# A hybrid encoder block on one core: casts and loads around the FFN's borders queued anew

## The chip, the cores and the metric

The kernel runs on one core of a Trainium2 chip. A core has five engines with a queue of instructions each: TensorE (PE in the profile, its weight loads PEld) multiplies matrices from SBUF into the PSUM banks; VectorE (DVE), ScalarE (ACT) and GpSimd (POOL) work elementwise; SyncE (SP) only issues DMA transfers. An engine takes its own instructions in the order in which the program was laid out; between engines, semaphores order them. The metric is the device time of one execution in microseconds, lower is better.

## The reference

One layer over 2048 tokens of width 1024, all in float32. Cut to what matters here:

```
h = rms_norm(x, pre_mix_g);  proj = h @ w_in
y_a = chunk_band_attention(q, k, v, rel_bias)
y_b = rwkv7_time_mix(p_rwkv, ...)
merged = sigmoid(gate_a) * (y_a @ proj_a) + sigmoid(gate_b) * (y_b @ proj_b)
x = x + rms_norm(merged @ w_out, post_mix_g)

hf = rms_norm(x, pre_ffn_g)
u = square(relu(hf @ w_up)) @ w_down        # 1024 -> 4096 -> 1024
x = x + rms_norm(u, post_ffn_g)
```

The change lies around the last four lines and the end of the line with w_out.

## The kernel before

**Splitting.** Each float32 operand of a matmul is split into a high part and a rest: `split` (L77) casts the high part on ACT (L78) and subtracts it from the source on DVE (L79). `split_here` (L1212) does the same with the rest left in the source's place (L1214, L1215). `mm3` multiplies high by high, high by rest and rest by high, three matmuls of 512 columns for each 128 rows of the contraction. So before PE can use an operand, a DMA has to land, a cast of 128x1024 has to run on ACT and a subtraction of the same size on DVE.

**Phases.** Four groups of 512 tokens go one after the other through the projections, the recurrence, attention and `phase_merge` (L1100). Then come two halves of 1024 tokens through the FFN: `phase_up`, `phase_down`, `phase_up`, `phase_down`.

**Merge.** `phase_merge` makes eight gated tiles: a product of 12 matmuls into a PSUM bank of the pool `pd` (two banks), its gating on DVE (`branch`, L1097), the sum with the other branch (L1114) and the split into `mh` and `ml` (L1115). The gate `th` comes by DMA into one of three buffers. Then `m @ w_out` runs in two halves of 512 columns (n = 0 and 1): eight steps k of 12 matmuls each into four banks, and at the end of a half ACT squares each bank (L1136) and DVE scales it by the norm row (L1137), after which the bank is free. The weights of w_out come as `wraw`, one load for two steps k.

**First activations.** `first_half` (L1218) loads the first token group's normalised activations for the FFN in four parts (`bl`) and splits them into `bh` and `bl`. For the first half it stands in the program behind the last merge, for the second half it is the last thing that the first `phase_down` advances beside its own work; there its casts are queued behind `self.second`, the weight cast of step 1.

**Up.** The FFN's two products use a form with seven block products in place of eight. `phase_up` (L1229) first runs eight blocks (`early`), each with a weight load, a split by `parts` (L1273) into one of the buffers a1, s12 and s3, a product A11 x B11 whose bank ACT copies to `z` (L1303), and a product A12 x B21 whose bank DVE adds to it (L1281); ACT then applies relu and square (L1282, L1283). Each product has 12 matmuls. Beside them the generator `operands` (L1251) loads and splits the five combined activations t2, t3, t1, b22 and t4 (two parts each), which the main loop needs. The main loop makes 16 passes; each splits S1 and S2 into s12, S3 and A22 into s3 and S4 into s4, and multiplies in the order S2, S3, S1, S4, A22. For passes below `early` the two first products exist already. The third block of the first half is the "third weights" of the title.

**Down.** `phase_down` (L1354) runs 56 steps, seven products of eight steps each; every step s needs one hidden block (`xraw`) and one weight block (`wdraw`), 512 KB each, from `operands(s)`, which is called two steps ahead. A step has 24 matmuls (L1409). `final` (L1426) closes a tile of 128 tokens: it loads the row tile `x1r` (two buffers), squares, scales by the norm row `gt` (a `gain` of 512 KB, L135), takes the root on POOL and adds. It is advanced from the sixth product on. The residual of the last token group (`residual`, L1140) runs beside the first down phase.

**Order.** The program is written in one order, but the order in each engine's queue is laid out at compile time by a planner: it takes an instruction as soon as, by its own estimates of time, its operands and buffers are ready and its engine is free, and prefers the one that stands earlier in the program. So a load, cast or subtraction of a later phase can be queued ahead of work that stands before it. `queue_behind(ins, first)` (L92) adds an edge for that planner alone: `ins` is laid out behind `first`. It adds no semaphore.

Of the kernel before, what the change touches and what calls it, by code (L numbers as in the profile page):

```python
# [18 lines left out]
P = 128  # L19
# [34 lines left out]
class Block:  # L54
# [79 lines left out]

    def gain(self, pool, src, name, bufs=1):  # L135
        t = pool.tile([P, D], F32, tag="gain", bufs=bufs, name=name)
        self.nc.sync.dma_start(t, src[None, :].to_broadcast((P, D)))
        return t

    def transpose_split(self, pt, src, hi, lo, tok, pinned=False):  # L140
# [959 lines left out]
    def phase_merge(self, g, o, op, between, beside):  # L1100

        tc, nc, a = self.tc, self.nc, self.a
        with ExitStack() as ctx:
            e = ctx.enter_context
            cp = e(tc.tile_pool(name="mgc", bufs=1, reuse_waits="tile"))
            po = e(tc.tile_pool(name="mgpo", bufs=4, space=PSUM, reuse_waits="tile"))
            mh = cp.tile([P, KB, G], F32R, name="mh")
            ml = cp.tile([P, KB, G], F32R, name="ml")
            gp = self.gain(op, a["post_mix_g"], "g_post")
            for i in range(KB):  # L1110
                mb = self.bp.tile([P, G], F32, tag="mb", bufs=3, name="mb")
                nc.sync.dma_start(mb, self.md[i])
                t = self.branch(self.ya, 0, i)
                nc.vector.tensor_tensor(t, t, mb, ALU.add)  # L1114
                self.split(mh[:, i], ml[:, i], t)  # L1115
            self.yctx.close()
            for n in range(2):
                ps = [po.tile([P, 512], F32, tag="o", name="ps_o") for _ in range(GT)]
                for k in range(KB):
                    if k % 2 == 0:  # L1120
                        w = a["w_out"][k * P : (k + 2) * P, n * 512 : (n + 1) * 512]
                        wh, wl = self.wsplit(w.rearrange("(j p) n -> p j n", p=P), "w", 2, 512)
                    for t in range(GT):
                        ts = slice(t * P, (t + 1) * P)
                        for j, (l, r) in enumerate(((mh, wh), (mh, wl), (ml, wh))):
                            nc.tensor.matmul(  # L1126
                                ps[t], l[:, k, ts], r[:, k % 2], start=k == 0 and j == 0, stop=k == KB - 1 and j == 2
                            )
                    if n == 0 and k in ((2, 4, 5, 6, 7) if g + 1 < self.NG else (0, 2, 3, 4, 5)):
                        advance(beside, 1)  # L1130
                    if n == 0 and k == 4 or n == 1 and k % 2 == 0:
                        advance(between, 1)
                ns = slice(n * 512, (n + 1) * 512)
                for t in range(GT):
                    sq = op.tile([P, 512], F32, tag="sqo", bufs=2, name="sqo")
                    nc.scalar.activation(sq, ps[t], AF.Square, accum_out=self.ssq[:, g, t, n : n + 1])  # L1136
                    nc.vector.tensor_tensor(o[t][:, ns], ps[t], gp[:, ns], ALU.mult)  # L1137
            advance(between)

    def residual(self, g, mp, bank):  # L1140
# [77 lines left out]
    def first_half(self, g, bp):  # L1218

        bh, bl = self.b1 = [bp.tile([P, KB, G], F32R, tag="b" + x, name="b" + x) for x in "hl"]  # L1220
        for k in range(0, KB, 2):
            ks = slice(k, k + 2)
            self.nc.sync.dma_start(bl[:, ks].bitcast(F32), self.ht[g][:, ks])
            high = self.split_here(bh[:, ks], bl[:, ks])
            if g:
                self.queue_behind(high, self.second)
            yield

    def phase_up(self, half, zp, rp, cb, pn, early):  # L1229
# [6 lines left out]
        with ExitStack() as ctx:  # L1236
# [14 lines left out]
            def operands():  # L1251
                td, g1 = self.td[half], self.ht[2 * half + 1]
                for n, src in (
# [3 lines left out]
                    for k in (0, 2):  # L1257
                        ks = slice(k, k + 2)
                        nc.sync.dma_start(l[:, ks].bitcast(F32), src[:, ks])
                        self.split_here(h[:, ks], l[:, ks])  # L1260
                        yield

            def product(l, r, pool, tag):
# [35 lines left out]

            ops = operands()  # L1300
            for i in range(early):
                A11, A12 = parts(load(2 * i), ("a1", "s12", "s3")[i % 3], KB)
                nc.scalar.copy(z[:, i], product(A11, B11, self.pd, "d"))  # L1303
                first(i, z[:, i])
                advance(ops, 1 + i % 2)
            advance(ops)

            last = None
# [45 lines left out]
    def phase_down(self, half, zp, rp, cb, pn, beside_of):  # L1354
# [4 lines left out]
        with ExitStack() as ctx:  # L1359
# [21 lines left out]
            def operands(s):  # L1381
# [5 lines left out]
                if isinstance(w, int):  # L1387
                    nc.sync.dma_start(wr, self.wd[w][f])
                else:
                    nc.sync.dma_start(wr, wrows[w[0]][:, 2 * f : 2 * f + 2, w[1]])  # L1390
                self.split(t[:, 0], t[:, 1], xr)
                high = self.split(t[:, 2], t[:, 3], wr)
                if s == 1:
                    self.queue_behind(self.relu, high)
                    self.second = high
                return t

# [28 lines left out]
            def final(t):  # L1426
                th = t // GT
                g, ts = gs[th], slice((t % GT) * P, (t % GT + 1) * P)
                x = op.tile([P, D], F32, tag="x", name="x1r")
                nc.sync.dma_start(x, self.x1[g][ts])  # L1430
                ssq = op.tile([P, 2], F32, tag="ssq", bufs=4, name="ssqu")
                for n in (1, 0):
                    ns = slice(n * G, (n + 1) * G)
# [19 lines left out]
            for s, (q, x, w, f) in enumerate(steps):  # L1453
# [9 lines left out]
                    continue  # L1463
                if s == NS - 3 * NF // 4 + 1:
                    gt = self.gain(op, a["post_ffn_g"], "g_post2")
                for t in range(GT):
                    down(ps[t], t, o, f == 0, f == NF // 4 - 1)
                    if f == NF // 4 - 1:
# [109 lines left out]
```

## Time and profile before

| | |
|---|---|
| median of 3 runs | 3269.18 us (3267.48 to 3270.03) |
| the profiled execution | 3272.55 us |
| its span, first to last instruction | 3270.8 us |
| mean granted clock of TensorE | 0.993 |
| first matmul of the first down phase | 2335.0 us |
| DMA moved | 592.54 MB, 181 GB/s over the span |

A line of the profile names the source line, the engine, the operation and the tiles as out<-in, with shapes and the number of instructions; a timeline line starts with the start and the duration in microseconds and ends, in brackets, with the idle time of the engine before the instruction and what ended it. Line numbers of helpers such as L78, L79 and L88 serve many callers, so tiles tell them apart: `a1h`, `s12h` and `s3h` are the split weights of the up phase, `t2h` to `t4h` and `b22h` its five operands, `bh` and `bl` the first activations, `fop` the operands of the down phase, `whi` and `wlo` the weights before the FFN.

### The profile page before, as it was taken

How to read it: one execution, taken by the hardware profiler on the slowest of the kernel's cores; microseconds unless marked ns; L12 is line 12 of the kernel's file. 1: busy time of each engine (PE TensorE's matmuls, PEld its weight loads, DVE VectorE, ACT ScalarE, POOL GpSimd, SP SyncE). 2: the span in 40 equal slices, each digit the busy share in tenths (PEclk: the TensorE clock that was granted, in tenths of full speed). 3: DMA queues.
4: the chain of work that ended last, by engine and by line, in shares of the span. 5: the costliest groups of instructions: out<-in, count | busy, mean ns of one | idle time of the engine just before them, and what ended most of it. 6: DMA issues, size and time to landing. Idle time of an engine off the chain costs nothing. (4 is left out here: it accounts for less than half of the span.)

```text
span 3270.8 us, 50026 instructions
## 1 busy us (share of the span) xinstructions
PE 3184.3 (97%) x18913; PEld 2599.2 (79%) x18913; DVE 2239.5 (68%) x3655; ACT 1576.9 (48%) x2511; POOL 596.0 (18%) x1101
## 2 busy tenths in 40 slices
PE   8999999999999999999999999999999999999998
PEld 6777778777888777878877887888888878888887
DVE  7785666776776785776866775887656768775464
ACT  5434635445745434755434653544543444544343
POOL 2221012122112222112222110122211212120000
PEclk9999999999999999999999999999999999999999
DMA  5245373246574236565336547654777875456565
GB/s 167 85 135 172 126 241 119 72 142 235 181 234 133 88 120 234 182 205 170 94 97 206 182 156 238 226 182 166 254 278 248 290 238 193 167 177 229 193 217 175
DMA packets 432282, 592.54 MB, mean 181 GB/s; under 512 B 25300, under 2 KB 295840, under 8 KB 432040
## 3 DMA queue, kind: packets, MB, share of 16 engines
q1 hardware_dynamic: 373928, 408.94, 39.9%
q0 software_dynamic: 48896, 163.61, 13.7%
q10 hardware_dynamic: 9216, 16.78, 1.4%
q8 instruction: 149, 2.44, 0.3%
q14 instruction: 93, 0.76, 0.1%
HBM read 425.37 MB, written 167.01 MB: 181 GB/s over the span
## 5 line engine op out<-in xcount | busy, mean ns | idle before, releaser
L1409 PE MATMUL ps_dn<-fop 128*128 128x512 f32 x2688 | 611.9, 389 | 1.8 <-DVE fop L79 1.7
L1409 PEld LDWEIGHTS ps_dn<-fop 128*128 128x128 f32 x2688 | 504.0, 188 | 107.8 <-DVE fop L79 2.8
L78 ACT CAST whi<-wraw 128x1024 fp32r<-128x1024 f32 x232 | 243.5, 1050 | 392.9 <-PE psd L88 301.1
L88 PE MATMUL psd<-hh,whi 128*128 128x512 f32 x1344 | 370.3, 403 | 10.7 <-DVE QA L894 10.7
L79 DVE TENSOR_TENSOR wlo<-wraw,whi 128x1024 fp32r<-128x1024 f32 x232 | 283.0, 1220 | 133.3 <-ACT whi L78 70.0
L88 PE MATMUL psd<-hl,whi 128*128 128x512 f32 x1344 | 367.2, 401 | 0.0
L88 PE MATMUL psd<-hh,wlo 128*128 128x512 f32 x1344 | 358.4, 398 | 0.0
L88 PEld LDWEIGHTS psd<-hh,whi 128*128 128x128 f32 x1344 | 244.8, 190 | 59.8 <-issue 11.8
L88 PEld LDWEIGHTS psd<-hl,whi 128*128 128x128 f32 x1344 | 249.1, 190 | 49.5
L88 PEld LDWEIGHTS psd<-hh,wlo 128*128 128x128 f32 x1344 | 247.9, 189 | 50.8 <-issue 1.4
L79 DVE TENSOR_TENSOR fop<-xraw,fop 128x1024 fp32r<-128x1024 f32 x112 | 137.0, 1224 | 178.9 <-ACT fop L78 178.7
L78 ACT CAST fop<-xraw 128x1024 fp32r<-128x1024 f32 x112 | 117.8, 1052 | 256.4 <-PE ps_dn L1409 186.3
L1286 POOL DMA_DIRECT2D xd<-X x192 | 104.2, 545 | 384.2 <-ACT X L1283 321.9
L79 DVE TENSOR_TENSOR fop<-wdraw,fop 128x1024 fp32r<-128x1024 f32 x112 | 136.6, 1220 | 19.0 <-ACT fop L78 18.8
L78 ACT CAST fop<-wdraw 128x1024 fp32r<-128x1024 f32 x112 | 117.7, 1051 | 34.8 <-DMA wdraw<-in_w_down_dram 20.0
L947 DVE CUSTOM_DVE_ANT_0 sc<-bias,ps_s 128x640 f32<-128x640 f32 (+4 forms) x128 | 93.8, 732 | 54.2 <-PE ps_pt L958 27.1
L963 DVE TENSOR_TENSOR PTl<-ps_pt,PTh 128x640 fp32r<-128x640 f32 (+4 forms) x128 | 94.5, 738 | 32.7 <-ACT PTh L962 31.2
L78 ACT CAST s12h<-s 128x1024 fp32r<-128x1024 f32 x32 | 33.7, 1053 | 163.0 <-PE ps_u L88 163.0
L88 PE MATMUL ps_p<-yh,whi 128*128 128x512 f32 x256 | 102.6, 405 | 6.0 <-DVE th L1097 5.3
L962 ACT CAST PTh<-ps_pt 128x640 fp32r<-128x640 f32 (+4 forms) x128 | 79.7, 623 | 55.2 <-PE ps_pt L958 54.6
L952 ACT ACTIVATE sc<-sc,mn 128x640 f32<-128x640 f32 (+4 forms) x128 | 97.8, 764 | 17.4 <-DVE mn L947 15.4
L1126 PE MATMUL ps_o<-whi,mh 128*128 128x512 f32 x256 | 101.4, 396 | 1.8 <-DVE o L1137 1.8
(369 smaller groups left out, 6848.9 us busy)
## 6 DMA issues: line engine op xcount, KB each, us to landing
wraw<-in_w_in_dram SPq DMA_DIRECT2D x168, 512.0 KB
xraw<-xd SPq DMA_DIRECT2D x112, 512.0 KB
xd<-X POOLq DMA_DIRECT2D x192, 256.0 KB, 5.2
wraw<-in_w_up_dram SPq DMA_DIRECT2D x80, 512.0 KB
wdraw<-wd SPq DMA_DIRECT2D x64, 512.0 KB
wdraw<-in_w_down_dram SPq DMA_DIRECT2D x48, 512.0 KB
gd<-gate ACTq DMA_DIRECT2D x64, 256.0 KB
wd<-cmb POOLq DMA_DIRECT2D x64, 256.0 KB, 4.3
```

The lines of the kernel that those rows point to most:

```text
L78: high = self.high = self.nc.scalar.copy(hi, src)
L79: self.low = self.nc.vector.tensor_tensor(lo, src, hi.bitcast(F32), ALU.subtract).ins
L88: mm.append(nc.tensor.matmul(ps, l, r, start=n == 0, stop=n == last).ins)
L947: nc.vector.tensor_tensor_reduce(sc[:, 0:n], bias[:, s0:640], pss[:, c0 : c0 + n], 1.0, 3.0e38, ALU.add, ALU.min, mn,)
L952: nc.scalar.activation(sc[:, 0:n], sc[:, 0:n], AF.Exp, scale=-1.0, bias=mn, accum_out=sm[:, col : col + 1])
L962: nc.scalar.copy(hv, pst[:, 0:nk])
L963: nc.vector.tensor_tensor(lv, pst[:, 0:nk], hv.bitcast(F32), ALU.subtract)
L1126: nc.tensor.matmul(ps[t], l[:, k, ts], r[:, k % 2], start=k == 0 and j == 0, stop=k == KB - 1 and j == 2)
L1286: nc.gpsimd.dma_start(self.xd[q][i // 2][:, i % 2], src)
L1409: nc.tensor.matmul(ps, o[:, l, k, sl], o[:, r, k], start=start and n == 0, stop=stop and n == end)
```

## The change

Six edits, all to the order that the planner lays out, apart from the choice of buffers:

1. The casts of the first activations for the first half are queued behind the merge's last cast (`self.merged`).
2. In the first half, cast and subtraction of the third block's weights are queued behind the last square and the last scaling of the half n = 0 of the last merge (`self.banks`).
3. The casts of the five operands are queued behind the copy of z of the block in which they are advanced (`copied`); they are advanced from the third block on, two parts a block, in place of one and two in turn from the first.
4. The eight early blocks take their split buffers in the turn a1, s12, s3, a1, s3, s12, s3, a1 in place of a1, s12, s3 repeated.
5. The casts of the first activations for the second half are queued behind the weight cast of step 5 of the first down phase in place of step 1.
6. In both down phases the loads of the closing rows (`x1r`) and of the norm row (`g_post2`) are queued behind the weight load of step 5 (`self.late`).

```diff
@@ gain
-        self.nc.sync.dma_start(t, src[None, :].to_broadcast((P, D)))
+        self.gained = self.nc.sync.dma_start(t, src[None, :].to_broadcast((P, D))).ins
@@ phase_merge
-                self.split(mh[:, i], ml[:, i], t)
+                self.merged = self.split(mh[:, i], ml[:, i], t)
...
-                    nc.scalar.activation(sq, ps[t], AF.Square, accum_out=self.ssq[:, g, t, n : n + 1])
-                    nc.vector.tensor_tensor(o[t][:, ns], ps[t], gp[:, ns], ALU.mult)
+                    squares = nc.scalar.activation(sq, ps[t], AF.Square, accum_out=self.ssq[:, g, t, n : n + 1])
+                    scaled = nc.vector.tensor_tensor(o[t][:, ns], ps[t], gp[:, ns], ALU.mult)
+                if n == 0:
+                    self.banks = squares.ins, scaled.ins
@@ first_half
-            if g:
-                self.queue_behind(high, self.second)
+            self.queue_behind(high, self.second if g else self.merged)
@@ phase_up, operands
-                        self.split_here(h[:, ks], l[:, ks])
+                        self.queue_behind(self.split_here(h[:, ks], l[:, ks]), copied)
@@ phase_up, early blocks
-                A11, A12 = parts(load(2 * i), ("a1", "s12", "s3")[i % 3], KB)
-                nc.scalar.copy(z[:, i], product(A11, B11, self.pd, "d"))
+                A11, A12 = parts(load(2 * i), ("a1", "s12", "s3", "a1", "s3", "s12", "s3", "a1")[i], KB)
+                if half == 0 and i == 2:
+                    for ins, done in zip((self.cast, self.low), self.banks):
+                        self.queue_behind(ins, done)
+                copied = nc.scalar.copy(z[:, i], product(A11, B11, self.pd, "d")).ins
                 first(i, z[:, i])
-                advance(ops, 1 + i % 2)
+                if i > 1:
+                    advance(ops, 2)
@@ phase_down, operands
-                    nc.sync.dma_start(wr, wrows[w[0]][:, 2 * f : 2 * f + 2, w[1]])
+                    load = nc.sync.dma_start(wr, wrows[w[0]][:, 2 * f : 2 * f + 2, w[1]])
+                    if s == 5:
+                        self.late = load.ins
...
                 if s == 1:
                     self.queue_behind(self.relu, high)
+                if s == 5:
                     self.second = high
@@ phase_down, final and main loop
-                nc.sync.dma_start(x, self.x1[g][ts])
+                self.queue_behind(nc.sync.dma_start(x, self.x1[g][ts]).ins, self.late)
...
                     gt = self.gain(op, a["post_ffn_g"], "g_post2")
+                    self.queue_behind(self.gained, self.late)
```

## The prediction

> **What bounds the kernel now.** I read three views in this order: the page's first part, the waits of TensorE (PE) from 1950 us on, where the change first acts, and the busy time by stretches.
>
> ```profile
> PE 3184.3 (97%) x18913; PEld 2599.2 (79%) x18913; DVE 2239.5 (68%) x3655; ACT 1576.9 (48%) x2511; POOL 596.0 (18%) x1101
> ```
>
> PE is busy for 97% of the span, and the change leaves its 18913 matmuls alone. So it can only remove waits, or add some. PE's waits after 1950 us (us in total, times, the longest) are these five groups and no others:
>
> ```profile
> PE ps_p L88 <- DVE th L1097: 2.5, 1, 2.5
> PE ps_u L88 <- ACT z L1303: 2.3, 3, 1.5
> PE ps_u L88 <- ACT s12h L78: 1.8, 2, 0.9
> PE ps_o L1126 <- DVE o L1137: 1.8, 1, 1.8
> PE ps_dn L1409 <- DVE fop L79: 1.7, 3, 0.8
> ```
>
> Ten waits, 2.5 + 2.3 + 1.8 + 1.8 + 1.7 = 10.1 us idle. Each costs more than its idle time, as PE's timeline around one of them shows:
>
> ```profile
> 2072.18 0.39 PE L88 MATMUL ps_u<-bl,s12h 128*128 128x512 f32 x1
> 2072.41 0.39 PE L88 MATMUL ps_u<-bh,s12l 128*128 128x512 f32 x1
> 2073.70 0.50 PE L88 MATMUL ps_u<-t2h,s12h 128*128 128x512 f32 x1 [0.91 <-ACT s12h L78]
> 2074.04 0.39 PE L88 MATMUL ps_u<-t2l,s12h 128*128 128x512 f32 x1
> ```
>
> Undisturbed starts lie 0.23 us apart (2072.18, 2072.41). The two steps around the wait took 1.63 us (2072.41 to 2074.04) instead of 0.46: an idle time of 0.91 costs 1.17, that is 0.26 more. Ten waits make 10.1 + 2.6 = 12.7 us. The two longest drag something further behind them; in the busy times by stretches, with granted clock, DMA share and GB/s at the end of each line:
>
> ```profile
> 1965.00:1975.00 10.00, 7.42 (x26) 5.52 (x25) 6.86 (x10) 3.13 (x4) 0.00 (x0) 0.83 0.91 310
> 1975.00:1985.00 10.00, 10.00 (x46) 8.26 (x45) 7.17 (x10) 3.76 (x5) 0.00 (x0) 1.00 0.87 302
> 2000.00:2010.00 10.00, 8.19 (x30) 6.28 (x29) 5.89 (x7) 5.35 (x11) 0.00 (x0) 0.83 1.12 320
> 2010.00:2020.00 10.00, 10.00 (x46) 8.29 (x45) 2.45 (x2) 2.11 (x2) 0.00 (x0) 1.00 0.05 19
> ```
>
> The waits in them:
>
> ```profile
> 1970.80 0.79 PE L88 MATMUL ps_p<-yh,whi 128*128 128x512 f32 x1 [2.54 <-DVE th L1097]
> ```
> ```profile
> 2004.39 0.50 PE L1126 MATMUL ps_o<-whi,mh 128*128 128x512 f32 x1 [1.81 <-DVE o L1137]
> ```
>
> The clock granted is 0.83 in both stretches with a wait and 1.00 in the ones behind them, and PE runs 26 and 30 matmuls (first count of a line) where 46 fit. The missing 20 and 16, at 0.23 us, are 4.6 and 3.7 us. Wait and restart explain 2.54 + 0.26 = 2.8 and 2.1 of it; the rest is the slow clock, 1.6 us in the second. Taking 1.6 for the first too, since it holds small losses beside, I put these places at 4.4 and 3.7 us. In all 12.7 + 3.2 = 15.9 us can be had.
>
> **First activations: the casts of bh behind the merge's last cast.** On ACT and DVE ahead of the wait of 2.54 us:
>
> ```profile
> 1967.24 1.05 ACT L1214 CAST bh<-bl 128x1024 fp32r<-128x1024 f32 x1 [3.80 <-DMA bl<-ht]
> 1968.20 0.61 ACT L78 CAST mh<-th 128x512 fp32r<-128x512 f32 x1
> ```
> ```profile
> 1968.32 1.23 DVE L1215 TENSOR_TENSOR bl<-bl,bh 128x1024 fp32r<-128x1024 f32 x1 [2.48 <-ACT bh L1214]
> ```
>
> A cast that only the FFN uses stands at ACT's head and waits for its DMA. Its subtraction holds DVE idle for 2.48 us, and behind that stands L1097, which frees the PSUM bank that PE wants. Held back, both leave, and the 4.4 us are won at this place. What is late next is a transfer:
>
> ```profile
> 1982.84 0.69 DVE L1097 SCALAR_TENSOR_TENSOR th<-th,ps_p 128x512 f32<-128x512 f32 x1 [2.15 <-DMA th<-gd]
> 1983.45 1.22 DVE L79 TENSOR_TENSOR wlo<-wraw,whi 128x1024 fp32r<-128x1024 f32 x1
> ```
>
> The last L1097 waits 2.15 us for its load already, with the split of an output weight behind it. If PE arrives sooner, these transfers must close up, and in the two stretches from 1965 on DMA has 0.09 and 0.13 of 10 us free: 2.2 us. The four bh casts also stand together behind the last cast now, one more than before (1.05 us on ACT, 1.23 on DVE), with w_out's casts behind them. The net lies between -1 (that extra cast, nothing won) and 4.4; I take the **2.2 us** by which DMA can close up. The loads of bl keep their place in SyncE's (SP's) queue.
>
> **Third weights: cast and subtraction behind the evacuation of the merge's first half.** On ACT, then on DVE:
>
> ```profile
> 2000.28 1.05 ACT L78 CAST s3h<-wraw 128x1024 fp32r<-128x1024 f32 x1 [3.15 <-DMA wraw<-in_w_up_dram]
> 2001.24 1.04 ACT L78 CAST whi<-wraw 128x1024 fp32r<-128x1024 f32 x1
> 2002.31 0.60 ACT L1136 ACTIVATE sqo<-ps_o 128x512 f32<-128x512 f32 x1
> ```
> ```profile
> 2001.37 1.23 DVE L79 TENSOR_TENSOR s3l<-wraw,s3h 128x1024 fp32r<-128x1024 f32 x1 [2.98 <-ACT s3h L78]
> 2002.51 1.22 DVE L79 TENSOR_TENSOR wlo<-wraw,whi 128x1024 fp32r<-128x1024 f32 x1
> 2003.64 2.48 DVE L1137 TENSOR_TENSOR o<-ps_o,g_post 128x512 f32<-128x512 f32 x4
> ```
>
> The s3h cast waits 3.15 us for a weight of the phase to come; behind it stand the cast of PE's next weights and the evacuation. With it moved, whi can start up to 3 us sooner, wlo follows, and each of the four L1137 (0.62 us) starts when its bank is done. PE's wait and its slow clock go: **3.7 us**, or half, 1.9, if w_out's own weights come late instead. The moved pair lies beside the 96 matmuls of the second half. One later load of w_up waits on SP for the raw buffer that it frees; DMA is at 0.05 after 2010, so that costs nothing.
>
> **Five operands: the T casts behind the copies of z.** On ACT, then on PE:
>
> ```profile
> 2661.65 1.05 ACT L1214 CAST t2h<-t2l 128x1024 fp32r<-128x1024 f32 x1 [3.33 <-DMA t2l<-td]
> ```
> ```profile
> 2663.75 0.50 PE L88 MATMUL ps_u<-bh,a1h 128*128 128x512 f32 x1 [1.46 <-ACT z L1303]
> ```
>
> ACT sits on t2h for 3.33 us, with the z copy that frees PE's bank behind it. Once the cast is behind the copy, its wait for DMA still blocks ACT, but what queues there is x's square and one weight split, and these have a block of PE (24 matmuls, 5.5 us) to spare. What is late next would be the last operand, t4:
>
> ```profile
> 2685.34 0.56 ACT L1303 COPY z<-ps_u 128x512 f32<-128x512 f32 x1
> ```
> ```profile
> 2692.95 0.50 PE L88 MATMUL ps_u<-t2h,s12h 128*128 128x512 f32 x1 [0.91 <-ACT s12h L78]
> ```
>
> It follows the copy at 2685.34 with two casts and two subtractions, some 4 us, and is first used four products (11 us) after 2692.95. So the three waits for z go: 2.3 + 3 x 0.26 = **3.1 us**; 1.5 if one half only obeys.
>
> **Split buffers in another turn.** The eighth block's weights lie in s12, where the main loop's first S1 and S2 are wanted at once. PE waits 0.91 us for it in each half (the row at 2692.95 and that at 2073.70). Afterwards s12's last early use is two blocks older. Tight next is s3 in the fifth and seventh block: the cast waits for the block two before, and 1.05 + 1.23 us must fit beside the one between, 5.5 us. That leaves room: **1.8 + 2 x 0.26 = 2.3 us**, or 1.2 if one of the two stays.
>
> **Step five's cast, norm row, closing rows.** SP's queue at the start of the first down phase, and ACT:
>
> ```profile
> 2339.30 0.38 SPq L1390 DMA_DIRECT2D wdraw<-in_w_down_dram  x1
> 2339.77 0.88 SPq L1430 DMA_DIRECT2D x1r<-x  x1
> ```
> ```profile
> 2350.45 1.05 ACT L78 CAST fop<-wdraw 128x1024 fp32r<-128x1024 f32 x1 [1.69 <-DMA wdraw<-in_w_down_dram]
> ```
> ```profile
> 2352.81 5.73 PE L1409 MATMUL ps_dn<-fop 128*128 128x512 f32 x24 [0.77 <-DVE fop L79]
> ```
>
> A weight issued at 2339.30 can be cast at 2350.45, 11 us later. The norm row stands ahead of it, a closing row behind it and so ahead of the next step's; in the second half the norm row and two closing rows (2954.57 below) go ahead of the operands.
>
> ```profile
> 2954.57 0.90 SPq L1430 DMA_DIRECT2D x1r<-x  x2
> ```
>
> Each is 512 KB, at the 310 GB/s of the stretch above 1.7 us, more than the 0.77 us that the longest wait idles. Behind step five's weight, they have left the way of the steps that wait; ahead of step six stand the same bytes as now, so it is no later; and their own first use is 40 steps on. The bh casts of the next half leave ACT here too. All three waits go: 1.7 + 3 x 0.26 = **2.5 us**, or 1.0 if the loads of the residual, which stay in front, suffice for a wait.
>
> **Sum.** 2.2 + 3.7 + 3.1 + 2.3 + 2.5 = 13.8, say 14 us. The profiled execution takes 3272.55 us, its span 3270.8, with 1.75 around it; it would take 3258.5. The median of the runs shown lies 3.4 us below it: 3269.2 - 14 = **3255**. The bounds: all terms full, 4.4 in place of 2.2, give 16.0; the lower ends -1 + 1.9 + 1.5 + 1.2 + 1.0 give 4.6. With 1.5 us for the spread of the runs: 3251.5 to 3266.
>
> **Rivals.**
>
> *The slow clock stays.* If the two dips have a cause beside these waits, 3.2 us aren't won: 3258. For it: an idle time of 1.81 us is short. Against: in both stretches the clock falls where the wait is. 7%. The Trainium skill, page "TensorE: Matmul & The Clock Gate", section "HAM oscillation — how this bites in real kernels", asks only that no idle gap pass some 3.4 us; by that rule neither wait would halve the clock and this rival holds. The trace speaks against it, with 0.83 granted beside 2.54 and 1.81 us of idle.
>
> *Other waits step in.* The order of ACT, DVE and SP is laid out anew behind each edit, and the transfers bind at all these borders. Then the next late transfer takes over the last three terms (7.9 us) and the first is given back whole; 0 to 6 us remain: 3263 to 3269. For it: DMA shares of 0.87 to 1.12 at the merge. Against: each held cast has a block of PE or more to spare. 13%.
>
> *Slower: the up loop takes the s12 wait into every pass.* ACT's waits in the same stretch:
>
> ```profile
> ACT s12h L78 <- PE ps_u L88: 166.0, 32, 7.1
> ```
>
> In all 32 passes of the two loops that cast waits for PE's last reader, and PE waits for it in two only. If the new order puts the sums that feed it a product later in every pass, PE pays 1.17 us 32 times, 37 us; from 12 passes on the 14 us are gone, and all of them give 3292. For it: the loop's order is laid out after the moved splits. Against: the pass itself isn't edited. 7%.
>
> **How the numbers follow.** Forecast 73%, slow clock 7%, other waits 13%, slower 7%. So faster by over 0.2% (6.5 us, about what a measurement of this kernel can tell from no change) 80%, within it 13%, slower 7%. The range leaves out the slower case, most of the other waits, and little else: 2 in 10.
>
> **What would show it.** Right: no bh cast before the merge's last mh; a granted clock of 1.00 through the merge; L1137 starting with PE's banks; no wait of PE for z, s12h or fop; g_post and x1r issued behind the sixth wdraw of a down phase. Wrong: new groups in PE's list of waits of 6 us together, above all behind loads of gd or w_out, or fewer than 46 matmuls in 10 us of an up loop.

## The result and the profile after

| | before | after |
|---|---|---|
| median | 3269.18 us, 5 runs (3267.48 to 3270.29) | 3255.72 us, 5 runs (3253.63 to 3258.3) |
| ratio, 95% interval | | 0.9961 (0.9946 to 0.9975) |
| the profiled execution, its span | 3272.55, 3270.8 us | 3253.63, 3251.9 us |

The kernel is 13.5 us faster by the medians; the interval of the ratio allows 8.2 to 17.7. The forecast was 3255.0 us. PE's share in the first part of the page of after:

```profile
PE 3174.1 (98%) x18913; PEld 2593.6 (80%) x18913; DVE 2238.6 (69%) x3655; ACT 1580.3 (49%) x2511; POOL 598.5 (18%) x1101
```

The same 18913 matmuls. PE's waits from 1950 us on, in total, times and the longest, of after:

```profile
PE ps_o L1126 <- DVE wlo L79: 1.2, 3, 0.6
PE ps_u L88 <- DVE x L1282: 1.2, 2, 1.0
PE ps_u L88 <- ACT z L1307: 0.9, 1, 0.9
PE ps_p L88 <- DVE th L1097: 0.5, 1, 0.5
PE ps_dn L1417 <- DVE fop L79: 0.2, 1, 0.2
```

Ten waits of 10.1 us have become eight of 4.0 us. The groups for s12h and for o are gone, th is down from 2.5 to 0.5 and fop from 1.7 to 0.2. Two groups are new: PE waits for the rests of w_out's weights (wlo), and for DVE's addition x. The merge by stretches of after, with clock, DMA share and GB/s at the end:

```profile
1960.00:1970.00 10.00, 10.00 (x45) 8.07 (x44) 8.21 (x13) 2.82 (x4) 0.00 (x0) 1.00 0.96 320
1970.00:1980.00 10.00, 9.64 (x43) 7.65 (x42) 8.70 (x12) 6.20 (x7) 1.08 (x2) 1.00 0.84 304
1980.00:1990.00 10.00, 9.11 (x39) 6.86 (x38) 8.16 (x9) 5.04 (x5) 1.08 (x2) 1.00 1.07 342
```

Granted clock 1.00 throughout, and DMA still at 0.84 to 1.07. What PE waits for there now has two causes. The first of the three waits for wlo (0.36 us) ends a chain that starts with a load of w_out. The longest (0.61 us) comes from DVE's order:

```profile
1977.28 1.05 ACT L78 CAST whi<-wraw 128x1024 fp32r<-128x1024 f32 x1
```
```profile
1977.70 2.36 DVE L1217 TENSOR_TENSOR bl<-bl,bh 128x1024 fp32r<-128x1024 f32 x2
1979.97 1.22 DVE L79 TENSOR_TENSOR wlo<-wraw,whi 128x1024 fp32r<-128x1024 f32 x1
```

The cast that wlo needs is done at 1978.33, but two subtractions of the first activations, whose casts the change has moved here, stand ahead of it on DVE.

Where the time went is read from PE's timeline, as differences between the starts of its first products in each part. In microseconds:

| from, to | before | after |
|---|---|---|
| start of the execution, last attention product | 1940.3 | 1932.0 |
| last attention product, first up product (merge) | 87.61 | 82.45 |
| up, first half: ahead of the loop | 45.81 | 43.52 |
| up loop, first half; second half | 261.27; 261.27 | 261.12; 261.12 |
| first down phase to the second up | 310.58 | 308.66 |
| up, second half: ahead of the loop | 47.40 | 47.15 |
| second down phase | 305.07 | 304.41 |
| behind it | 11.53 | 11.54 |

From the last attention product on, after is 10.6 us shorter (1330.5 and 1320.0). The 8.3 us ahead of it need another explanation: no instruction stands in another order there. In the second half's up head, from which three waits were to go (1.46, 0.39 and 0.91 us idle in before, 3.5 us with their restarts), 0.25 us are won.

### The profile page after: what moved, and what is told of

Its sections match the earlier page's. It is cut to its first block, busy times and chain, and to the rows that moved or that the text cites. A ratio compares the mean times of both kernels' runs of the same rounds, so it can differ in the third digit from the quotient of the medians.

```text
span 3251.9 us, 50021 instructions
## 1 busy us (share of the span) xinstructions
PE 3174.1 (98%) x18913; PEld 2593.6 (80%) x18913; DVE 2238.6 (69%) x3655; ACT 1580.3 (49%) x2511; POOL 598.5 (18%) x1101
## 3 DMA queue, kind: packets, MB, share of 16 engines
q0 software_dynamic: 48896, 163.61, 13.8%
## 5 line engine op out<-in xcount | busy, mean ns | idle before, releaser
L88 PEld LDWEIGHTS psd<-hh,whi 128*128 128x128 f32 x1344 | 245.8, 191 | 60.2 <-issue 11.8
L1126 PE MATMUL ps_o<-wlo,mh 128*128 128x512 f32 x256 | 100.4, 392 | 2.7 <-DVE wlo L79 2.7
```

The source lines that it names most:

```text
L88: mm.append(nc.tensor.matmul(ps, l, r, start=n == 0, stop=n == last).ins)
L1126: nc.tensor.matmul(ps[t], l[:, k, ts], r[:, k % 2], start=k == 0 and j == 0, stop=k == KB - 1 and j == 2)
```

## The experiments

Each kernel was run on the chip with a profile; no_late_again and weights_pinned with more executions, the others with one. Because the part ahead of the last attention product varies by chance, each is read by its stretches. All are in this table (merge, the heads of the two up phases, the first and second down phase, as above), with the number of stretches of 3.4 us with a granted clock of 0.50 in the part ahead (the last section shows one; two in a row count as two), and the time at which that part ends:

| kernel | merge | head 1 | down 1 | head 2 | down 2 | slow stretches ahead | ahead ends |
|---|---|---|---|---|---|---|---|
| before | 87.61 | 45.81 | 310.58 | 47.40 | 305.07 | 9 | 1940.3 |
| after | 82.45 | 43.52 | 308.66 | 47.15 | 304.41 | 5 | 1932.0 |
| no_first | 83.59 | 43.54 | 308.35 | 46.97 | 304.41 | 8 | 1936.0 |
| no_third | 83.17 | 43.64 | 309.05 | 46.83 | 304.41 | 8 | 1938.0 |
| no_ops | 80.90 | 44.43 | 308.38 | 47.31 | 304.41 | 10 | 1938.0 |
| old_turn | 81.09 | 44.65 | 308.67 | 47.88 | 304.41 | 6 | 1935.0 |
| no_late | 80.82 | 43.52 | 313.37 | 47.03 | 305.04 | 10 | 1939.4 |
| no_late_again | 80.71 | 43.62 | 310.35 | 46.86 | 304.67 | 8 | 1936.1 |
| hold_rests | 81.47 | 43.52 | 308.25 | 45.46 | 304.41 | 8 | 1938.0 |
| hold_eighth | 82.30 | 43.55 | 308.32 | 46.27 | 304.41 | 8 | 1937.5 |
| hold_both | 81.17 | 43.52 | 308.50 | 48.59 | 304.41 | 5 | 1934.0 |
| weights_first | 81.65 | 43.53 | 308.81 | 47.70 | 304.41 | 6 | 1932.4 |
| weights_rests | 81.08 | 43.52 | 308.33 | 46.61 | 304.41 | 9 | 1935.2 |
| weights_pinned | 83.28 | 43.52 | 308.29 | 43.78 | 304.41 | 5 | 1933.2 |

Eleven of these kernels have the merge of after; its mean there is 81.54 us (80.71 to 83.28), so after's own 82.45 is one of the longer ones, and the change is worth 6.1 us at this place, not 5.2.

### First activations put back

```diff
-            self.queue_behind(high, self.second if g else self.merged)
+            if g:
+                self.queue_behind(high, self.second)
```

> The first activations' casts stand where they stood in the kernel before; all else is as in the changed kernel. Measured from the last product of the attention part to the merge's first product with w_out, which took 40.4 us before and 36.75 us after. Theory (the cast's wait for its DMA holds DVE, and so PE's bank): 40.4 us again, with a wait of PE for th of 2 to 2.6 us and a lower granted clock behind it; the three waits for w_out's weights behind it (1.25 us idle together after) go, since the DMA has that much more time. From there to the second half of the merge 0.5 to 1 us less than the 23.94 after. Rival (the merge is bound by its DMA, and the wait for th is only where that shows): 37 to 38 us, or the gain is given back whole by the start of the second half: 60.7 us from the last attention product to there, as after, within 0.5 us. By the theory it is 63 to 64 us.

PE's timeline of this kernel, and its stretch around that row:

```profile
1966.12 0.50 PE L88 MATMUL ps_p<-yh,whi 128*128 128x512 f32 x1 [2.18 <-DVE th L1097]
```
```profile
1960.00:1970.00 10.00, 7.69 (x26) 5.59 (x25) 7.54 (x11) 3.13 (x4) 0.00 (x0) 0.83 0.91 300
```

The wait and the lower clock are back, at the same product. Up to the first product with w_out it took 40.07 us, as before (40.37); the eleven take 35.81 to 38.14, 36.4 in the mean. But then the three waits for wlo are missing, and the first half of w_out takes 21.76 us where after took 23.94, a larger return than the 0.5 to 1 us expected. At its own place the edit is worth 3.7 us; over the whole merge 83.59 - 81.54 = 2.1. To the start of the second half it was 61.8 us, between the 63 to 64 of the theory and the 60.7 of the rival: somewhat under half is given back, to the waits for wlo. One of 0.5 to 0.6 us is in all eleven kernels, each time with two of the moved subtractions ahead of it on DVE; the rest, where there is more, mostly follows a late load of w_out. So the merge's DMA is only a part of what is given back.

### Third weights put back

```diff
-                if half == 0 and i == 2:
+                if False:
```

> The third weights' cast and subtraction stand where they stood in the kernel before; all else is as in the changed kernel. Theory (the wait of this cast for its weight holds the cast of PE's next weights and the evacuation of the banks): the wait of PE at the start of the merge's second half returns, 1.5 to 1.9 us idle, and the half takes 23.5 us as before in place of 21.76, or 21.9 if the clock stays at 1.00 behind this wait; the three waits for w_out's weights in the first half (1.25 us) stay. Rival (the wait came from the late evacuation that the first activations' casts had put off, and went with them): the second half takes 21.8 us and shows no wait over 0.5 us. In all 1.5 to 3.7 us more by the theory from the last attention product to the up phase's first product, 0 by the rival.

Two of PE's waits in the merge, and the stretch with the longer:

```profile
PE ps_o L1126 <- DVE o L1137: 1.7, 1, 1.7
PE ps_o L1126 <- DVE wlo L79: 1.0, 2, 0.6
```
```profile
1990.00:2000.00 10.00, 8.32 (x36) 6.30 (x35) 6.91 (x8) 6.44 (x13) 0.00 (x0) 1.00 1.13 335
```

The wait returns, so it is this cast and its subtraction that made it, and the rival falls. The clock stayed at 1.00 behind it: 83.17 - 81.54 = 1.6 us, without the 1.6 us of slow clock that stood beside the same wait before.

### Five operands not held

The edge from the operands' casts to the copy of z is left out; their later start from the third block on is kept.

```diff
-                        self.queue_behind(self.split_here(h[:, ks], l[:, ks]), copied)
+                        self.split_here(h[:, ks], l[:, ks])
```

> The casts of the five T operands are not held behind the copies of z; the turn of the split buffers and all else is as in the changed kernel. Theory (ACT sits on a T cast that waits for its DMA, with the z copy behind it): PE's waits for z return, one or two in the first half (0.3 to 0.6 us each) and one of 1.2 to 1.5 us in the second, but the wait of 0.97 us for DVE's x in the second half goes, since the DVE subtractions move with the casts: first half's up head 44.5 to 45 us (43.52 after), second half's 47 us (47.15 after), that is no change there: the edit trades one wait for another. Rival (the z waits come from the weights' own casts, by the turn of the buffers): both heads stay within 0.3 us of after and the wait of 0.97 us stays.

PE's waits of this kernel:

```profile
PE ps_u L88 <- ACT z L1307: 2.0, 2, 1.6
PE ps_u L88 <- DVE x L1282: 1.2, 1, 1.2
```

The waits for z are back, 0.4 us in the first half and 1.6 in the second. The first head takes 44.43 us in place of 43.52, the second 47.31 in place of 46.97 (the mean of the five executions with after's second head: after, no_first, no_third, no_late and no_late_again). So the edge is worth 0.9 + 0.3 = 1.2 us; the 0.3 is no more than the spread of those five (46.83 to 47.15). That the wait for x would vanish was wrong in this form: it stayed, one of 1.2 us some 24 us later in the head.

### Split buffers in the old turn

```diff
-                A11, A12 = parts(load(2 * i), ("a1", "s12", "s3", "a1", "s3", "s12", "s3", "a1")[i], KB)
+                A11, A12 = parts(load(2 * i), ("a1", "s12", "s3")[i % 3], KB)
```

> The split buffers take their old turn (a1, s12, s3 again and again); all else is as in the changed kernel. Theory: PE waits 0.9 us for s12h once in each half again, 1.17 us of time each; in the second half the wait of 0.85 us for z goes, since the eighth block's cast is then held by the sixth block's last reader and doesn't sit on ACT ahead of the z copy. First half's up head 44.7 us (43.52 after), second half's 47.15 + 1.17 - 1.1 = 47.2 us. Rival (the new turn costs nothing, and the wait of 0.85 us for z comes from the T casts behind it): second half's head 48.3 us, with the wait for z still there.

```profile
PE ps_u L88 <- ACT s12h L78: 1.8, 2, 0.9
...
PE ps_u L88 <- ACT z L1307: 0.8, 1, 0.8
```

These are two of PE's wait groups. The waits for s12h are back, and the heads take 1.13 and 0.91 us more; each loop takes 261.26 in place of 261.12 us, 0.28 for both. The sum is 2.3 us. The second head's 47.88 lies between the theory's 47.2 and the rival's 48.3: the wait for z stayed, so the new turn doesn't cause it; I had held that it does. Here the block that stands in its way is split into s12 and not a1; what the two kernels share is that its weight lands late (the cast waits 3.71 us for it here, 2.65 in after).

### Norm row and closing rows loaded where they were

Step five's cast as anchor (edit 5) is kept, edit 6 is undone. This kernel ran twice, the second time with ten executions.

```diff
-                self.queue_behind(nc.sync.dma_start(x, self.x1[g][ts]).ins, self.late)
+                nc.sync.dma_start(x, self.x1[g][ts])
...
-                    self.queue_behind(self.gained, self.late)
```

> The norm row and the closing rows are loaded where they were in the kernel before; step five's cast as anchor of the next half's casts, and all else, are as in the changed kernel. Theory (these loads stand ahead of the weights of the steps that wait): PE's waits for fop return in the second down phase, two of them, and that phase takes 305.0 to 305.1 us as before in place of the 304.41 that every kernel with the held loads took; the first down phase, 308.35 to 309.05 in the five kernels so far, takes 309.5 to 310.6 (before: 310.58). Rival (the first down phase's 1.9 us came from the next half's casts, not from the loads): second phase 305.05, first 308.4 to 309.0 with at most one wait for fop.

> The norm row and the closing rows loaded where they were in the kernel before, the same kernel as the earlier look at it, which showed a first down phase of 313.37 us (before 310.58, changed kernel 308.66) with a wait of 2.2 us and a lower clock behind it. Theory (the transfers ahead of step five are over their limit there by a fixed amount, and the place of those loads alone decides): first down phase 311.5 to 313.5 us again, time 3260 to 3265 us, 5 to 9 us above the changed kernel's. Rival (the 2.2 us were one execution's chance): 309.5 to 310.6 us and 3257 to 3259 us.

ACT's and PE's rows of the first run, and of the second:

```profile
2342.41 1.04 ACT L78 CAST fop<-wdraw 128x1024 fp32r<-128x1024 f32 x1 [2.10 <-DMA wdraw<-in_w_down_dram]
...
2343.51 0.51 PE L1417 MATMUL ps_dn<-fop 128*128 128x512 f32 x1 [2.17 <-ACT fop L78]
```
```profile
2337.66 1.04 ACT L78 CAST fop<-wdraw 128x1024 fp32r<-128x1024 f32 x1 [3.13 <-DMA wdraw<-in_w_down_dram]
...
2338.76 0.50 PE L1417 MATMUL ps_dn<-fop 128*128 128x512 f32 x1 [0.73 <-ACT fop L78]
```

In both, the cast of a step's weights waits for its transfer, and PE for the cast. The first down phase took 313.37 and 310.35 us, against a mean of 308.51 in the eleven kernels with the held loads (308.25 to 309.05), the second 305.04 and 304.67 against 304.41 in all of them. The wait is caused by these loads; its size, 2.17 or 0.73 us, differs between two executions of one kernel, and with the longer one came a slow stretch of clock. The median of the ten executions is 3257.52 us (3252.69 to 3262.26), beside a kernel before with a median of 3265.55 on the same chip, a ratio of 0.9976 (0.9967 to 0.9986); after had 0.9961. By the stretches edit 6 is worth 1.8 + 0.3 = 2.1 us in the second execution, as the rival of the second expectation had it, and 4.9 + 0.6 in the first, of which up to 1.7 is the slow clock. The times don't decide between 2 and 5: the medians of this kernel and of after lie 1.8 us apart, the ratios 0.0015, which is 4.9 us, and their intervals overlap. The edge of edit 5 wasn't undone by itself.

### The second half's head

Why did it not fall to the first's 43.5 us? The timeline of after:

```profile
2643.91 1.05 ACT L1216 CAST t2h<-t2l 128x1024 fp32r<-128x1024 f32 x1 [1.53 <-DMA t2l<-td]
2644.99 2.51 DVE L1217 TENSOR_TENSOR t2l<-t2l,t2h 128x1024 fp32r<-128x1024 f32 x2 [3.84 <-ACT t2h L1216]
...
2647.42 0.68 DVE L1282 TENSOR_TENSOR x<-z,ps_u 128x512 f32<-128x512 f32 x1
...
2648.15 0.50 PE L88 MATMUL ps_u<-bh,a1h 128*128 128x512 f32 x1 [0.96 <-DVE x L1282]
...
2660.13 1.05 ACT L78 CAST a1h<-wraw 128x1024 fp32r<-128x1024 f32 x1 [2.65 <-DMA wraw<-in_w_up_dram]
2661.08 0.63 ACT L1283 ACTIVATE x<-x 128x512 f32<-128x512 f32 x1
...
2661.74 0.63 ACT L1284 ACTIVATE x<-x 128x512 f32<-128x512 f32 x1
2662.28 0.57 ACT L1307 COPY z<-ps_u 128x512 f32<-128x512 f32 x1
...
2662.90 0.50 PE L88 MATMUL ps_u<-bh,s3h 128*128 128x512 f32 x1 [0.85 <-ACT z L1307]
```

There are two things to see. The cast of t2 stands behind the copy of z now, but its subtraction on DVE wasn't given an edge: DVE idles 3.84 us for it, and the addition that frees PE's bank stands behind. And on ACT the cast of the eighth block's weight waits 2.65 us for its DMA, with relu, square and the copy of z behind it. Three kernels hold back the one, the other and both.

```diff
+                        self.queue_behind(self.rest, self.added)       # hold_rests, hold_both: in operands()
...
+                if i == 7:
+                    self.queue_behind(self.cast, copies[5])            # hold_eighth, hold_both: in the early blocks
```

> Added to the changed kernel: the DVE subtractions of the T operands are queued behind the latest block's DVE addition, as the casts already are behind the copy of z. Theory (the five operands' edit moved only the casts; their subtractions stand in DVE's queue ahead of the addition that frees PE's bank): PE's wait of 0.97 us for x in the second half's up head goes, 1.2 us of time; the wait for z of 0.7 to 0.9 us stays; the second head takes 45.7 us (46.83 to 47.15 in the kernels with this order so far), the first 43.5 as after. Rival (the addition is late for another reason, its own block's cast or PE's): the wait stays and the head takes 46.8 to 47.2 us.

> Added to the changed kernel: the eighth block's weight cast is queued on ACT behind the sixth block's copy of z. Theory (that cast stands on ACT 1.8 to 3.7 us waiting for its weight, ahead of the relu, the square and the z copy that frees PE's bank; seen with the old turn of the buffers too): PE's wait of 0.7 to 0.9 us for z in the second half goes, 1.0 us of time, the wait for x stays: second head 45.9 us, first 43.5. Rival (the weight itself is what PE needs next, so that the wait comes back one block later behind the cast): the wait for z becomes one for a1h and the head stays at 46.8 to 47.2 us.

> Both additions at once. Theory: the second half's up head comes down to the first's, 43.5 to 44.0 us, some 3.2 us below the changed kernel's: the five operands' edit would then have brought in both halves what was forecast for it. Rival (the transfers of the T operands, issued together, bind the second half's head whatever the queues do): 45.5 us or more, with PE's waits for t2h, t3h or a1h instead.

PE's waits in ps_u, of hold_rests and then of hold_eighth (line numbers shift by up to four with each kernel's edit):

```profile
PE ps_u L88 <- ACT z L1308: 1.3, 1, 1.3
```
```profile
PE ps_u L88 <- DVE x L1282: 1.8, 2, 1.1
```

Each removes the wait that it was made for: 45.46 and 46.27 us in place of 46.97. In the first, the wait for z grew from 0.7 to 0.9 us to 1.3; in the second, a second wait for x came in its place, and the head lies between its theory's 45.9 us and its rival's 46.8. With both, the head is the longest of all, 48.59 us, of which up to 1.7 us are a slow stretch of clock. DVE and PE of that kernel, and the stretch behind the wait:

```profile
2664.35 0.69 DVE L1332 TENSOR_TENSOR s<-wraw 128x512 f32<-128x512 f32 x1 [4.22 <-DMA wraw<-in_w_up_dram]
...
2666.29 0.68 DVE L1283 TENSOR_TENSOR x<-z,ps_u 128x512 f32<-128x512 f32 x1
...
2667.03 0.50 PE L88 MATMUL ps_u<-bh,s3h 128*128 128x512 f32 x1 [2.92 <-DVE x L1283]
```
```profile
2667.00:2672.00 5.00, 4.97 (x15) 3.98 (x16) 4.79 (x5) 4.23 (x6) 0.54 (x1) 0.66 0.19 65
```

The planner filled the places that came free: three operations on the loop's first weights now stand ahead of the sixth block's addition on DVE, where after has one. They wait 4.22 us for their load, and the addition behind them. So the theory of two queues was too small. What this wait and the one for z have in common is a weight that lands late. SP's queue in after says why:

```profile
2637.10 0.38 SPq L1271 DMA_DIRECT2D wraw<-in_w_up_dram  x1
...
2643.96 1.59 SPq L1260 DMA_DIRECT2D t4l<-td  x2
2647.16 15.68 SPq L1271 DMA_DIRECT2D wraw<-in_w_up_dram  x5
```

Behind the load at 2637.10 stand ten loads of operands, 512 KB each. The eighth block's weight is issued at 2647.16, and the cast that waits for it starts at 2660.13, 13.0 us later. The last operands, t4, aren't used until the loop is four products in.

### The weights' loads ahead of the last operands

```diff
+                if half and i == 0:                        # main loop, all three kernels
+                    for ins in moved[6:]:                  # the loads of b22 and t4
+                        self.queue_behind(ins, self.loaded)
...
+                        self.queue_behind(self.rest, self.added)       # weights_rests, weights_pinned
...
+                if half and i == 7:                        # weights_pinned
+                    self.queue_behind(self.cast, copies[4])
...
+                if half and i == 0:                        # weights_pinned: first sum of S1
+                    self.queue_behind(total, adds[5])
```

> Added to the changed kernel, in the second half alone: the loads of the last two T operands (b22 and t4, four loads of 512 KB) are queued on SP behind the loads of the eighth block's weight and of the main loop's first pair, instead of ahead of them. Theory (the second half's head is bound by the place of the weights in SP's queue: ten operand loads stand ahead of them, and whichever of ACT and DVE works on a weight waits and holds PE's bank): the eighth block's weight lands some 5 us sooner (12.9 us from issue to landing in the changed kernel), PE's wait for z goes, the wait for x of 0.97 us, which the subtractions of t2 cause, stays: second head 45.8 to 46.1 us in place of 46.8 to 47.15. Rival (the transfers' sum decides, not their order): the same wait returns behind b22 or t4, 46.8 us or more.

> The same, and the DVE subtractions of the T operands queued behind the latest block's addition. Theory: both waits gone, second head 43.5 to 44.2 us as the first, 3 us below the changed kernel's. Rival (DVE's sums of the loop's weights, which wait for their loads, come ahead of an addition as when both holds were put in, 2.9 us): 46 us or more with a wait of PE for x.

> As the last kernel with the weights' loads ahead of b22 and t4 and the subtractions behind the additions, and in the second half two more edges: DVE's first sum of the loop's weights behind the sixth block's addition, and the eighth block's weight cast behind the fifth block's copy of z. Theory (each of PE's waits in this head came from an instruction that waits for a load and stands ahead of the one that frees the bank; with loads and queues both ordered nothing is left): no wait of PE over 0.3 us in either head, second head 43.5 to 43.9 us, from the last attention product to the end 1312.5 to 1314.5 us (1319.97 changed kernel, 1330.5 before); median of the times 3.0 to 3.5 us below that of the changed kernel against the same kernel before: ratio 0.9950 to 0.9955, with executions spread over some 8 us by the part ahead. Rival (the wait moves once more, to the first product of the loop behind S1 and S2): 45 to 46.5 us with a wait for s12h.

PE's waits in the up heads, of the first and then of the second kernel:

```profile
PE ps_u L88 <- DVE x L1282: 3.0, 3, 1.8
```
```profile
PE ps_u L88 <- DVE x L1283: 1.6, 1, 1.6
...
PE ps_u L88 <- ACT z L1309: 0.4, 1, 0.4
```

Both miss what the theory expected of them (47.70 and 46.61 us, where 45.8 to 46.1 and 43.5 to 44.2 were expected): with the loads moved, the planner takes casts and sums for these weights still earlier, and they stand ahead of an addition again, as the second's rival had it. (The first is also in the range of its own rival, 46.8 us or more, but with waits for x, not behind b22 or t4.) With the loads and both queues ordered, the waits go. Whether the two queues with the edge on the sum would do it without the loads wasn't tried. All of PE's waits from 1950 us on in weights_pinned:

```profile
PE ps_p L88 <- DVE th L1097: 1.1, 1, 1.1
PE ps_o L1126 <- DVE wlo L79: 0.6, 1, 0.6
```

None is left in either up head, and the second takes 43.78 us, 3.2 less than the changed kernel's mean. From the last attention product to the end it took 1317.1 us, not the 1312.5 to 1314.5 that I wrote: that sum was wrong, since 3.4 us less in the head make 1316.6 of after's 1320.0, and its merge was the longest of the eleven. In 6 executions the median is 3252.78 us (3248.31 to 3257.49) beside 3265.89 (3260.18 to 3271.25) for the kernel before on the same chip: ratio 0.9960 (0.9946 to 0.9974), above the 0.9950 to 0.9955 expected, and not to be told from after's 0.9961. It removes the waits; that it is faster than after is shown by the stretch alone, not by the times.

## Why the prediction was right, point by point

The sum was 13.8 us. By stretches, with the means of the kernels that share the stretch, it is 6.1 in the merge, 2.3 in the first head, 0.4 in the second, 0.3 in the loops, 2.1 and 0.7 in the down phases: together 11.8 us before rounding, against one execution of before. The medians differ by 13.5, with an interval from 8.2 to 17.7 that holds both. That the median came within 0.7 us of the forecast is in part luck: two terms measured under half of their forecasts (the third weights without the slow clock), and the kernel before had medians of 3265.55 and 3265.89 us in the 13 and 11 executions beside later kernels, not the 3269.18 from which the forecast started.

| term | predicted | measured | by |
|---|---|---|---|
| first activations | 2.2 net, 4.4 at the place | 2.1 net, 3.7 at the place | no_first |
| third weights | 3.7 | 1.6, and up to 1.6 for the clock | no_third |
| five operands | 3.1 | 1.2 | no_ops |
| split buffers | 2.3 | 2.3 | old_turn |
| step five, norm row, closing rows | 2.5 | 2.7 | stretches of after and before |

The rows add up to 9.9 us; with the clock's 1.6 it is 11.5.

**First activations.** Right in the wait and in its price at the place. The net of 2.2 us came out, but not for the reason given. The forecast limited the gain by how far the transfers can close up; the longest wait that came in its place, 0.5 to 0.6 us in all eleven kernels, is for a wlo behind the moved subtractions on DVE. The prediction named that extra work (1.05 us on ACT, 1.23 on DVE) and used it only for its lower bound.

**Third weights.** The wait was right, and 1.9 to 2.0 us with its restart was its price. The other 1.6 us, the slow clock, was priced as if it followed from every such wait. It followed in before, and not in no_third. It is a term with a chance: behind the attention part, a slow stretch followed one of the five waits of 1.55 to 1.81 us in these traces, and all four of 2.17 to 2.92 us. The last section shows what goes with it.

**Five operands.** The step that failed is this one: "Once the cast is behind the copy, its wait for DMA still blocks ACT, but what queues there is x's square and one weight split, and these have a block of PE (24 matmuls, 5.5 us) to spare." It followed ACT's queue and left out DVE's, where the cast's own subtraction stands ahead of the addition that frees the other bank: an edge on a cast doesn't move the instruction that depends on it away from what stands behind it. hold_rests, which adds that edge, shortens the second head by 1.5 us. The "one weight split" didn't have its block to spare either: the eighth block's cast waits 2.65 us for its load with the copy of z behind it, and hold_eighth, which moves it away, shortens the head by 0.7 us. In the first half the T loads land nearly in time (the cast of t2 waits 0.20 us for its load in after, 1.53 in the second half), and the term was not far off there: 0.9 us by no_ops, of 1.3 forecast (0.8 us of waits and two restarts).

**Split buffers.** Right in the wait, and the sum to a tenth, with 0.3 of it in the loops rather than at their start.

**Step five, norm row, closing rows.** Right: 2.1 + 0.7 us, with one wait for fop of 0.2 us left of three. no_late shows that the place of these loads makes the wait; what edit 5 adds wasn't tried alone.

**The rivals.** That the slow clock stays: no slow stretch is left in the merge of after. Two stretches with waits of 1.6 to 1.8 us, no_third's at 1.00 above and this one of weights_first, with a wait of 1.77 us in it, kept a full clock:

```profile
2660.00:2665.00 5.00, 4.28 (x19) 3.55 (x20) 5.00 (x7) 4.26 (x7) 0.54 (x1) 1.00 0.90 279
```

Against them stand no_first (2.18 us idle, 0.83 granted) and hold_both (2.92 us, 0.66), as in before (2.54 and 1.81 us). By the rule of the Trainium skill, page "TensorE: Matmul & The Clock Gate", section "HAM oscillation — how this bites in real kernels", that only gaps over some 3.4 us count, none of these four would have shown one; here the measurement decides. That other waits step in: they did, but the two new groups (wlo and x) make 2.4 us of the 4.0 that remain of 10.1, at the merge and the second head alone. That the loop takes the s12 wait into every pass: no, 261.12 us against 261.27, and no wait for s12h.

**The base.** The forecast took 3.4 us off for the median, since before's profiled execution was above it. The table suggests what that was: nine slow stretches ahead, more than most, and two more in the merge.

## What to carry to other kernels

An edge that holds back one instruction must be followed on every engine that its result passes through: the cast left ACT's way and its subtraction took DVE's. A planner that fills freed slots draws the next late transfer's work forward, so first ask which load lands late and what stands ahead of it in the DMA queue; here each hold on a queue alone shortened the head, by 1.5 and 0.7 us, and both together without the loads lost that again (1.6 us longer than without them, by a wait of 2.9 us and a slow clock behind it); the loads without the queues made it 0.7 us longer, and loads and queues together 3.2 us shorter. Read an edit by the stretch that it touches: the parts it doesn't touch moved by up to 8.3 us between executions here, more than any one edit was worth.

## What was not expected of the hardware

The slow clock comes in pieces, and on a grid. The same wait of PE, in before and then in after, with stretches of 3.41 us around it:

```profile
143.10 0.66 PE L643 MATMUL ps_at<-ident,AR 128*128 128x128 f32 x4 [2.35 <-ACT XT L628]
```
```profile
141.17:144.58 3.41, 1.37 (x28) 1.14 (x30) 0.86 (x2) 3.33 (x7) 0.18 (x1) 1.00 0.55 159
144.58:148.00 3.42, 3.42 (x28) 2.46 (x25) 1.06 (x1) 1.17 (x2) 0.36 (x1) 0.50 0.00 0
```
```profile
143.94 0.66 PE L643 MATMUL ps_at<-ident,AR 128*128 128x128 f32 x4 [2.35 <-ACT XT L628]
```
```profile
139.55:142.96 3.41, 2.04 (x40) 1.47 (x33) 3.31 (x5) 2.37 (x4) 0.00 (x0) 1.00 0.03 9
142.96:146.37 3.41, 2.31 (x39) 1.92 (x40) 0.00 (x0) 2.85 (x7) 0.18 (x1) 1.00 0.51 150
```

Both waited 2.35 us; in before the clock then was 0.50 for 3.4 us, in after 1.00. Such a stretch, if it is all matmuls, loses 1.7 us. Over the 14 executions of the table the part ahead held 5 to 10 of them, and its length follows that number with a correlation of 0.84 and 1.2 us for each. The four fewer in after go with some 5 of the 8.3 us by which it was ahead of before at the last attention product; what made the rest stays open. Executions of one kernel spread over 5 to 11 us.

What goes with such a stretch can be read from the traces. In each execution all slow stretches start on one grid of 3.413 us, to within 0.003 us (104 stretches between 25 and 3230 us), and the grid lies elsewhere in the kernel in each execution. Behind the attention part, where nearly all matmuls have 512 columns, five windows of that grid had PE busy for 26, 28, 36, 38 and 47% of the time, and a slow stretch followed each; no other window there was under 50%, and no other was followed by one. So what counts here is how much of a wait falls into one window. Of the wait above, 1.9 us lie in one window in before (PE busy 1.37 of 3.41 us, 40%) while in after it is split into 1.4 and 1.0 us (60 and 68%). In no_third the window with the wait had 51%, in before, with nearly the same wait, 47%. In the part ahead, with its smaller matmuls, the border is less sharp: all windows under 43% were followed by a slow stretch, and some up to 69% (windows already at the slow clock apart). These are readings of the traces; no kernel was made to test them.
